# Strassen's seven block products for the first MLP product of a two-layer trunk

## The chip, the cores and the metric

The kernel runs on one core of one Trainium2 chip. Its time is that of one execution on the device, in microseconds (us). The core has five engines that run side by side and meet through semaphores: PE (TensorE, matrix products into the eight banks of PSUM), DVE (VectorE), ACT (ScalarE), POOL (GpSimd) and SP (SyncE, which here only issues DMA transfers between DRAM and the on-chip memory SBUF). DVE and ACT read PSUM and SBUF; POOL works on SBUF alone. A tile is 128 partitions by so many columns, and 512 columns of float32 fill one bank.

## The reference: what is computed

A trunk of two layers works on 1024 positions (tokens) with 1024 features. Layer 0 mixes positions with two recurrent head groups, layer 1 with chunked attention. The rest of a layer is the same for both and is what this change touches:

```
x = x + mix                                   # mix ends in an output projection, 1024 x 1024
hf = rmsnorm(x, norm_ffn_g[i])
x = x + jnp.square(jax.nn.relu(hf @ mlp_w1[i])) @ mlp_w2[i]     # 1024 -> 4096 -> 1024
x = x + rmsnorm(p[i] @ ple_w_proj[i], ple_norm_g[i]) * jax.nn.sigmoid(x @ ple_w_gate[i])
```

The two products of the MLP are each 1024 x 1024 x 4096. The norm's factor per position (rs) can be applied after the first product, since it scales whole positions.

## The kernel before

Everything is kept transposed: features on the partitions, positions on the columns. x is eight tiles of 128 features by 1024 positions, and each is worked on in two halves of 512 positions.

**A product in three.** Float32 operands are split into a high part, rounded to a format that PE multiplies in one pass (float32r), and a low part, the rest. `mm3` (line 276) forms high x high, high x low and low x high: three matmuls of 128x512 for each step of 128 in the sum. A weight tile comes as 512 KB by DMA (`load_w`, line 262) into a buffer `wraw`; ACT casts it to `whi` (line 272), DVE subtracts that to get `wlo` (line 273). `dense_part` (line 288) runs eight (or four) such steps into one PSUM bank and hands it to a function that evacuates it.

**The tail of a layer** is `tail` (line 1152). x is loaded whole into eight SBUF tiles. The output projection runs over its eight output tiles n; the half of the earlier positions is done before, and here only the later half remains, one bank each (tiles 0 and 1 come finished in `self.first`). Its evacuation `ev_out` adds the bank to x, splits x times the norm's weight into the operand `xg` (`split_scaled`, line 309) and adds up the squares of x (`sumsq`, line 320: ACT squares, POOL accumulates).

The MLP goes in eight groups of four tiles of hidden features. `mlp1(g)` makes group g: per tile 2 halves x 8 steps x 3 = 48 matmuls; the evacuation takes the positive part times rs (DVE, line 1222), squares it into the high part (ACT, 1223), squares it again in float32 (POOL, 1224) and subtracts for the low part (DVE, 1225). `mlp2(g)` multiplies the four tiles by the second weights and adds into x (DVE, 1239): 16 banks of 4 x 3 = 12 matmuls. The order is mlp1(0), mlp1(1), mlp2(0), mlp1(2), mlp2(1) and so on; hidden tiles never leave SBUF. Then come the gate's product and the final addition (lines 1265 to 1275).

**What sets the order.** Each engine runs its own queue in order. The order in a queue is made when the program is built: a scheduler goes through time with a model of how long instructions take and, on each engine, issues the earliest instruction of the program that is ready by that model. Buffers are rings: a new tile in a ring waits until all uses of the tile that held the place are done. The first rows of positions' factors (`row_stats`, `to_rows`) are placed by hand after the first and second evacuation of the MLP.

Of the kernel before, what the change touches and what calls it, by code (L numbers as in the profile page):

```python
# [8 lines left out]
F32 = mybir.dt.float32  # L9
F32R = mybir.dt.float32r  # L10
# [7 lines left out]
P = 128  # L18
# [86 lines left out]
class Trunk:  # L105
# [1048 lines left out]
    def tail(self, i, xsrc):  # L1154
        nc, tc, a = self.nc, self.tc, self.a
        V, A, G = nc.vector, nc.scalar, nc.gpsimd
        last = i == 1
        with ExitStack() as es:
# [3 lines left out]
            self.wp = es.enter_context(self.pool(f"wpt{i}", 2))  # L1162
            x = [self.xp.tile([P, 3, T], F32, tag=f"xw{q}", name=f"xw{q}") for q in range(2)]
            x = [x[k // 3][:, k % 3, :] for k in range(6)]
            x += [self.xp.tile([P, T], F32, tag=f"x{k}", name=f"x{k}") for k in (6, 7)]
            self.ht = es.enter_context(self.pool(f"ht{i}"))
            self.sm = es.enter_context(self.pool(f"smt{i}", 2))
            self.slots = {"f": (self.ht, 3)}
            if i == 1:
                self.pre = es.enter_context(self.pool("pre1"))  # L1170
            rs = [None]
            nr = [0]

            def actR():
                q = nr[0] % 8
                nr[0] += 1
                return (self.rx if i == 0 and q < 4 else pB).tile([P, 2, T], F32R, tag=f"r{q}", name="r")

            def actA():
                return self.actA.tile([P, 2, T], F32R, tag="a", name="a")  # L1180

            bt, at = (actR, actA) if i == 0 else (actA, actR)
            hs = [slice(0, HB), slice(HB, T)]
            for k in range(NK):
                nc.sync.dma_start(out=x[k][:, HB:T], in_=xsrc[k][:, HB:T])
            for k in range(NK):
                nc.sync.dma_start(out=x[k][:, 0:HB], in_=self.xh[k])
            accs = [self.accp.tile([P, HB], F32, tag=f"acc{hf}", name="acc") for hf in range(2)]
            col = self.cst.tile([P, NT], F32, tag="col", name="col")
            xg = [at() for _ in range(NK)]  # L1190

            def ev_out(n):
                def f(ps):
                    V.tensor_tensor(x[n][:, hs[1]], x[n][:, hs[1]], ps, op=ALU.add)
# [4 lines left out]
            for n in range(NK):  # L1199
                if n < 2:  # L1200
                    ev_out(n)(self.first[n])
                else:
                    w = self.w_next if (i, n) == (0, 2) else self.load_w(a[f"w_out{i}"][n])
                    yield from self.dense_part(w, self.y, ev_out(n), self.order)

            def rows():
                rs[0] = self.pre.tile([P, T], F32, tag="ph", name="rs")
                self.to_rows(col, rs[0])

            self.late, self.plan = [], {1: lambda: self.row_stats(accs, col), PLAN_ROWS: rows}  # L1210

            xf = [None] * NK

            def mlp1(g):
                hid = []
                for j in range(4):
                    h = bt()
# [535 lines left out]
```

## Time and profile before

| | |
|---|---|
| median of 3 runs | 3310.28 us (3301.96 to 3310.35) |
| profiled execution, its own time | 3307.32 us |
| its span, first to last instruction | 3305.6 us |
| mean granted TensorE clock | 0.972 |
| MLP stages | about 1008 to 1712 (layer 0) and 2510 to 3210 (layer 1) |

How to read the lines of the profile below. PE, PEld (weight loads, which overlap the products), DVE, ACT, POOL and SP are the engines; a q after the name is the engine's sequencer. A group reads: line of the kernel, engine, operation, output<-inputs, shapes, xcount, then busy us and mean ns of one, then idle time just before and what ended it. The answer for one line of the kernel gives the durations as min/median/max in ns and the first and last start. The table of stretches gives for each the busy us of each engine with the number of instructions in brackets, the granted clock (PEclk), the share of DMA engines busy and GB/s. In a timeline the first two columns are start and duration in us. Durations include time in which an engine that has begun an instruction is held up.

### The profile page before, as it was taken

Reading aid. Unit: us, or ns where it says so; the run is one execution under the profiler, and the core shown is the slowest. Engines: PE = TensorE matmul, PEld = TensorE weight load, DVE = VectorE, ACT = ScalarE, POOL = GpSimd, SP = SyncE. Lnnn points to the kernel's source line nnn. Section 1 sums busy time; section 2 is a strip of 40 time slices with the busy share of each in tenths; the row PEclk is TensorE's granted clock in tenths of the full one; section 3 lists DMA queues with packets and bytes.
Section 4 is the critical chain, followed back from the end, with each engine's and each line's share of the span. In section 5 each row is a group of like instructions: output and inputs, shape, how many; then the busy total and the mean of one; then the engine's idle time right before and its main releaser. Section 6 shows DMA issues by size and latency. Waiting matters only on the chain.

```text
span 3305.6 us, 46018 instructions
## 1 busy us (share of the span) xinstructions
PE 3197.8 (97%) x17960; PEld 2639.7 (80%) x17960; DVE 1720.1 (52%) x3550; ACT 1054.5 (32%) x2040; POOL 930.9 (28%) x1262
## 2 busy tenths in 40 slices
PE   7999999999999999999999998889899999999999
PEld 5777777877778888888887988889678888888887
DVE  5566665657554333333357667666854333333344
ACT  4333333334332111111123555555642111111121
POOL 6333533345312101111115335444523111111102
PEclk8999899999889999999999999999999999999999
DMA  3311111222341111111114011010352111111113
GB/s 117 98 60 51 55 55 60 63 69 95 130 138 51 51 45 51 45 51 45 52 64 148 32 44 40 31 34 18 112 204 66 49 46 51 46 51 46 51 46 121
DMA packets 105547, 221.51 MB, mean 67 GB/s; under 512 B 36593, under 2 KB 38769, under 8 KB 105329
## 3 DMA queue, kind: packets, MB, share of 16 engines
q1 hardware_dynamic: 105328, 218.57, 20.0%
q8 instruction: 141, 2.31, 0.3%
q14 instruction: 78, 0.63, 0.1%
HBM read 181.83 MB, written 36.70 MB: 66 GB/s over the span
## 4 chain that ended last, share of the span: by engine, by line
PE 90%; DVE 6%; ACT 2%; issue 1%; DMA 1%; POOL 1%; SPq 0%; DVEq 0%; ACTq 0%; POOLq 0%
PE dps L161 73%; PE ch L161 3%; PE iz L161 2%; PE po L161 2%; PE pm L161 2%; PE tp L161 1%; PE pt L165 1%; PE sn L161 1%; PE py L161 1%; DVE ptile L314 1%; PE pp L161 1%; PE sc L161 1%; PE sf L161 1%; PE dps L165 0%; PE st L161 0%
## 5 line engine op out<-in xcount | busy, mean ns | idle before, releaser
L161 PE MATMUL dps<-a,whi 128*128 128x512 f32 x2304 | 723.3, 394 | 0.0
L161 PE MATMUL dps<-r,whi 128*128 128x512 f32 x2304 | 710.1, 389 | 0.0
L272 ACT CAST whi<-wraw 128x1024 fp32r<-128x1024 f32 x233 | 244.6, 1050 | 1016.7 <-PE dps L161 792.5
L161 PEld LDWEIGHTS dps<-a,whi 128*128 128x128 f32 x2304 | 431.1, 187 | 105.8
L161 PEld LDWEIGHTS dps<-r,whi 128*128 128x128 f32 x2304 | 432.2, 188 | 90.0
L161 PE MATMUL dps<-xg,whi 128*128 128x512 f32 x1360 | 461.7, 416 | 8.4 <-ACT xg L316 7.3
L1224 POOL TENSOR_TENSOR f<-f 128x512 f32<-128x512 f32 x128 | 160.1, 1252 | 1080.2 <-ACT r L1223 541.4
L161 PE MATMUL dps<-a,wlo 128*128 128x512 f32 x1152 | 454.3, 394 | 0.0
L161 PE MATMUL dps<-r,wlo 128*128 128x512 f32 x1152 | 448.2, 389 | 0.0
L273 DVE TENSOR_TENSOR wlo<-wraw,whi 128x1024 fp32r<-128x1024 f32 x233 | 295.3, 1268 | 91.8 <-ACT whi L272 91.6
L161 PEld LDWEIGHTS dps<-xg,whi 128*128 128x128 f32 x1360 | 263.0, 198 | 74.1 <-issue 10.7
L161 PE MATMUL dps<-wq,a 128*128 128x384 f32 x1536 | 304.0, 345 | 5.3 <-DVE vs L1503 3.1
L1239 DVE TENSOR_TENSOR xw<-xw,dps 128x512 f32<-128x512 f32 x192 | 132.0, 688 | 302.5 <-PE dps L161 302.3
L161 PE MATMUL dps<-xg,wlo 128*128 128x512 f32 x680 | 280.9, 413 | 3.1 <-DVE wlo L273 3.1
L161 PEld LDWEIGHTS dps<-wq,a 128*128 128x128 f32 x1536 | 267.0, 191 | 10.4 <-DVE vs L1503 5.3
L1611 POOL TENSOR_SCALAR pb<-pb,l 128x640 f32<-128x640 f32 (+4 forms) x128 | 193.7, 1519 | 248.7 <-DVE l L1610 149.4
L161 PEld LDWEIGHTS dps<-a,wlo 128*128 128x128 f32 x1152 | 215.7, 187 | 53.1
L161 PEld LDWEIGHTS dps<-r,wlo 128*128 128x128 f32 x1152 | 216.2, 188 | 45.0
L1222 DVE SCALAR_TENSOR_TENSOR f<-dps,rs 128x512 f32<-128x512 f32 x128 | 88.3, 691 | 266.3 <-PE dps L161 263.7
L161 PEld LDWEIGHTS dps<-xg,wlo 128*128 128x128 f32 x680 | 133.9, 197 | 35.8 <-issue 4.8
L161 PE MATMUL po<-ptile,vs 128*128 128x256 f32 (+1 forms) x576 | 109.4, 301 | 21.2 <-DVE ptile L314 8.9
L1268 POOL TENSOR_TENSOR pn<-pn,prs 128x512 f32<-128x512 f32 x32 | 48.7, 1524 | 263.2 <-ACT prs L350 177.0
(443 smaller groups left out, 4498.7 us busy)
## 6 DMA issues: line engine op xcount, KB each, us to landing
wraw<-in_w SPq DMA_DIRECT2D x128, 512.0 KB
wraw<-in_w_in SPq DMA_DIRECT2D x56, 512.0 KB
wraw<-in_w_out SPq DMA_DIRECT2D x32, 512.0 KB
wraw<-in_w_qkv SPq DMA_DIRECT2D x24, 512.0 KB
pn<-pnd SPq DMA_DIRECT2D x32, 256.0 KB
wraw<-in_w_gate SPq DMA_DIRECT2D x16, 512.0 KB
yr<-yd SPq DMA_DIRECT2D x30, 256.0 KB
xr<-in_x SPq DMA_DIRECT2D x8, 512.0 KB
```

The costliest lines, as they stand in the source:

```text
L161: return self.nc.tensor.matmul(out, lhsT, rhs, start=start, stop=stop)
L165: return self.nc.tensor.transpose(out, in_, ident)
L272: nc.scalar.copy(hi, raw)
L273: nc.vector.tensor_tensor(lo, raw, hi.bitcast(F32), op=ALU.subtract)
L314: nc.vector.tensor_tensor(dst[:, 1, sl], src, dst[:, 0, sl].bitcast(F32), op=ALU.subtract)
L1222: V.scalar_tensor_tensor(t, ps, 0.0, rs[0][:, sl], op0=ALU.max, op1=ALU.mult)
L1224: G.tensor_tensor(t, t, t, op=ALU.mult)
L1239: V.tensor_tensor(x[n][:, sl], x[n][:, sl], ps, op=ALU.add)
L1268: G.tensor_tensor(pn, pn, prs[:, sl], op=ALU.mult)
L1611: G.tensor_scalar(pb[:, 0:(nf + nn) * P], pb[:, 0:(nf + nn) * P], l[:, 2:3], None, op0=ALU.mult)
```

## The change

The first MLP product is done in pairs of output tiles. A pair's result is cut in 2 x 2 blocks (two tiles of hidden features by two halves of positions), the sum over 1024 features in two halves (even and odd tiles, four steps each). Eight block products would be 8 x 4 x 3 = 96 matmuls; Strassen's method needs seven (84 matmuls), each of a combination of weight blocks with a combination of input blocks, and adds the results up.

- *Inputs.* The seven combinations of the input blocks are built once per layer in `ev_out` and `first_half`, for each couple of x tiles (even and odd), and split into high and low parts: `cmb[1]` to `cmb[7]`. x is no longer held whole: two tiles at a time are loaded (`load_x`), the later half is stored back to DRAM (`xh2`) after the addition, the squares for the norm overwrite the tile. Scaled x goes through one tile `xs` of four quarters.
- *Weights.* `raws(p)` loads the two weight tiles of pair p; `prepare(p, m)` builds combination m in place on POOL (five of the seven need a sum) and splits it on ACT and DVE. It is written one pair ahead.
- *Results.* `product(p, m)` runs 12 matmuls into a bank. ACT copies three of the seven banks out, DVE adds the other four to what is there, POOL does four more sums. Each of the four blocks is then taken to its positive part times rs (DVE), squared (ACT) and stored to DRAM (`hd`).
- *Second product.* It is a stage of its own after all pairs. Squares are loaded back 512 KB at a time and split again (`load_hidden`), four tiles ahead; weights one tile ahead (`load_w2`). x is loaded again from `xh` and `xh2` at the start of that stage.
- *Around it.* The PSUM ring grows from 6 to 8 banks. The pools for weights and evacuation in the tail go; their tiles come from one ring of six tiles (`act`), two more with tag "b", and four tiles called late. Gate weights are loaded after the tile before the last, not ahead of each tile.

The diff, cut to its core:

```diff
+    def act(self, shape, dt, tag="a"):
+        return self.actA.tile(shape, dt, tag=tag, name="act", bufs=6 if tag == "a" else 2)
...
-            self.psd = 2 * self.psd[0:1] + 4 * [es.enter_context(self.pool(f"psdt{i}", 4, space=PSUM))]
+            self.psd = 2 * self.psd[0:1] + 6 * [es.enter_context(self.pool(f"psdt{i}", 6, space=PSUM))]
...
+            def split(c, s):
+                hi, lo = c[:, 0], c[:, 1]
+                if len(s.shape) > 2:
+                    hi, lo = (z.rearrange("p (j c) -> p j c", c=P) for z in (hi, lo))
+                A.copy(hi, s)
+                V.tensor_tensor(lo, s, hi.bitcast(F32), op=ALU.subtract)
...
+            def load_x(n):
+                nc.sync.dma_start(out=xr[n % 2][:, hs[1]], in_=xsrc[n][:, hs[1]])
+                nc.sync.dma_start(out=xr[n % 2][:, hs[0]], in_=self.xh[n])
+
+            def scaled(n, hf):
+                A.activation(xs[:, n % 2, hs[hf]], xr[n % 2][:, hs[hf]], AF.Copy, scale=self.vec("ffng", 8 * i + n))
+            b11, b12, b21, b22 = quarters(xs)
+
+            def first_half(n):
+                scaled(n, 0)
+                if n % 2:
+                    j = n // 2
+                    split(cmb[2][j], b11)
+                    V.tensor_tensor(b21, b21, b11, op=ALU.subtract)
+                    split(cmb[4][j], b21)
 
             def ev_out(n):
                 def f(ps):
-                    V.tensor_tensor(x[n][:, hs[1]], x[n][:, hs[1]], ps, op=ALU.add)
+                    t, j = xr[n % 2], n // 2
+                    V.tensor_tensor(t[:, hs[1]], t[:, hs[1]], ps, op=ALU.add)
+                    nc.sync.dma_start(out=self.xh2[n], in_=t[:, hs[1]])
+                    scaled(n, 1)
+                    if n % 2:
+                        split(cmb[5][j], b22)
+                        V.tensor_tensor(b22, b22, b11, op=ALU.add)
+                        G.tensor_tensor(b12, b12, b11, op=ALU.add)
+                        split(cmb[1][j], b22)
+                        V.tensor_tensor(b11, b12, b22, op=ALU.subtract)
+                        split(cmb[3][j], b11)
+                        split(cmb[6][j], b12)
+                        G.tensor_tensor(b21, b21, b22, op=ALU.add)
+                        split(cmb[7][j], b21)
                     for hf in range(2):
-                        self.split_scaled(xg[n], x[n][:, hs[hf]], self.vec("ffng", 8 * i + n), hs[hf])
-                        self.sumsq(accs[hf], x[n][:, hs[hf]], n == 0)
+                        if n:
+                            A.activation(t[:, hs[hf]], t[:, hs[hf]], AF.Square)
+                            G.tensor_tensor(accs[hf], accs[hf], t[:, hs[hf]], op=ALU.add)
...
+            order = (4, 2, 5, 3, 1, 6, 7)
+            def raws(p):
+                r = place(F32)
+                for e in (1, 0):
+                    nc.sync.dma_start(out=r[:, e], in_=a["w1"][i, 2 * p + e])
...
+                o, u, v, op = {4: (a22, None, None, None), 5: (a12, a12, a11, ALU.add), 2: (a21, a21, a22, ALU.add),
+                               3: (a11, None, None, None), 1: (a22, a22, a11, ALU.add), 6: (a21, a21, a22, ALU.subtract),
+                               7: (a12, a12, a22, ALU.subtract)}[m]
+                if u is not None:
+                    G.tensor_tensor(o, u, v, op=op)
+                split(d[m], o)
...
+            def product(p, m):
+                ps, c = self.bank(), prep[p][1][m]
                 for j in range(4):
+                    o, z = slice(j * P, j * P + P), cmb[m][j]
+                    self.mm3(ps, c[:, 0, o], c[:, 1, o], z[:, 0], z[:, 1], j == 0, j == 3)
+                return ps
...
+            def hidden(t, k, hf):
+                V.scalar_tensor_tensor(t, t, 0.0, rs[:, hs[hf]], op0=ALU.max, op1=ALU.mult)
+                A.activation(t, t, AF.Square)
+                nc.sync.dma_start(out=self.hd[k][:, hs[hf]], in_=t)
...
+            for p in range(16):
+                k = 2 * p
+                if p < 15:
+                    raws(p + 1)
+                for m in order:
+                    ps = product(p, m)
...
+                    if m in (4, 5, 1):
+                        c = scr()
+                        A.copy(c, ps)
+                    if m == 4:
+                        m4 = c
+                    elif m == 2:
+                        c21 = scr()
+                        V.tensor_tensor(c21, m4, ps, op=ALU.add)
+                    elif m == 5:
+                        m5 = c
+                        plus(G, m4, m5, ALU.subtract)
+                    elif m == 3:
+                        plus(V, m5, ps)
+                        f = scr()
+                        G.tensor_tensor(f, m5, c21, op=ALU.subtract)
+                        hidden(c21, k + 1, 0)
+                        hidden(m5, k, 1)
+                    elif m == 1:
+                        plus(G, m4, c)
+                        plus(G, f, m4)
+                    elif m == 6:
+                        plus(V, f, ps)
+                        hidden(f, k + 1, 1)
+                    else:
+                        plus(V, m4, ps)
+                        hidden(m4, k, 0)
+                    if p < 15:
+                        prepare(p + 1, m)
+                    elif m == 5:
+                        load_w2(0)
+                        for j in range(3):
+                            load_hidden(j)
...
+            x = tiles_x(F32)
+            for k in range(NK):
+                nc.sync.dma_start(out=x[k][:, hs[0]], in_=self.xh[k])
+                nc.sync.dma_start(out=x[k][:, hs[1]], in_=self.xh2[k])
...
+            def mlp2(g):
+                hid = H[g % 2]
                 for n2 in range(4):
-                    hi, lo = self.load_w(a["w2"][i, g, n2])
+                    q = 4 * g + n2
+                    hi, lo = w2.pop(q)
+                    if q < 31:
+                        load_w2(q + 1)
+                    if g < 7:
+                        load_hidden(q + 4)
```

More of the change, by code (lines that the diff above doesn't have):

```diff
@@ L1179, in actA @@
[L1179 to L1187, printed above, removed]
+            pB = [pB.tile([P, 2, T], F32R, tag=f"r{q}", name="r") for q in range(8)]
@@ new lines, in tail, with place, lates @@
+            late = es.enter_context(self.pool("late1")) if last else self.rx
+            if last:
+                self.pre = es.enter_context(self.pool("pre1"))
+            self.sm = es.enter_context(self.pool(f"smt{i}", 2))
+            def place(dt, far=False, tag="a"):
+                if far:
+                    return late.tile([P, 2, T], dt, tag=tag, name="late")
+                return self.act([P, 2, T], dt, tag)
+            def lates(dts):
+                return [place(dt, True, f"r{q}") for q, dt in enumerate(dts)]
@@ new lines, in ring, with f, tiles_x @@
+            def ring(views):
+                state = [0]
+                def f():
+                    state[0] += 1
+                    return views[(state[0] - 1) % len(views)]
+                return f
+            halves = lambda t: [t[:, q, :] for q in range(2)]
+            quarters = lambda t: [t[:, q, hs[e]] for q in range(2) for e in range(2)]
+            two = lambda t: t.rearrange("p (q c) -> p q c", q=2)
+            parts = lambda t: [two(v) for v in halves(t)]
+            def tiles_x(dt):
+                xw = [self.xp.tile([P, 3, T], dt, tag=f"xw{q}", name=f"xw{q}") for q in range(2)]
+                return ([xw[k // 3][:, k % 3, :] for k in range(6)] +
+                        [self.xp.tile([P, T], dt, tag=f"x{k}", name=f"x{k}") for k in (6, 7)])
@@ new lines, in tail @@
+            xv = [two(v) for v in tiles_x(F32R)]
+            pq = [c for t in pB for c in parts(t)]
+            cmb = {4: pq[0:4], 2: pq[4:8], 5: xv[0:4], 3: xv[4:8], 1: pq[8:12], 6: pq[12:16],
+                   7: [c for _ in range(2) for c in parts(place(F32R, tag="b"))]}
+            if last:
+                wo, wr, wo2, xr = lates([F32R, F32, F32R, F32])
+            else:
+                wo, wr, wo2, xr = (place(dt) for dt in (F32R, F32, F32R, F32))
+            xs = place(F32)
+            wo, wr, xr = [wo, wo2], halves(wr), halves(xr)
@@ new lines, in weights @@
+            def weights(src, raw, hl):
+                nc.sync.dma_start(out=raw, in_=src)
+                split(hl, raw)
+                return hl[:, 0], hl[:, 1]
+            def load_x(n):
[3 more added lines that the diff above has]
+                A.activation(xs[:, n % 2, hs[hf]], xr[n % 2][:, hs[hf]], AF.Copy, scale=self.vec("ffng", 8 * i + n))
@@ L1258, in tail @@
                 self.xd = [self.dr.tile([P, T], F32, tag=f"xd{k}", name="xd") for k in range(NK)]
-                xg = [at() for _ in range(NK)]
+            scr = ring(quarters(lt[3]))
             def ev_gate(n):
@@ L1417, in load_w @@
             return hi, lo
-        p = [act([P, 2, T], F32R) for _ in range(2)]
+        p = [act([P, 2, T], F32R, "b") for _ in range(2)]
         acc = act([P, 2, HB], F32)
@@ L1459, in load_qkv @@
         for j in range(3):
-            raw = pool.tile([P, T], F32, tag="wraw", name="wraw")
+            raw = place()
             nc.sync.dma_start(out=raw, in_=self.a["w_qkv"][pr, j])
```

134 lines of the change are left out of this document (82 added, 52 removed).

## The prediction, made before the changed kernel was run

> **What bounds the kernel now.** First the page: busy time, the span in slices, the chain of waits.
>
> ```profile
> span 3305.6 us, 46018 instructions
> PE 3197.8 (97%) x17960; PEld 2639.7 (80%) x17960; DVE 1720.1 (52%) x3550; ACT 1054.5 (32%) x2040; POOL 930.9 (28%) x1262
> ...
> PE   7999999999999999999999998889899999999999
> PEclk8999899999889999999999999999999999999999
> ...
> PE 90%; DVE 6%; ACT 2%; issue 1%; DMA 1%; POOL 1%; SPq 0%; DVEq 0%; ACTq 0%; POOLq 0%
> ```
>
> PE carries 90% of the chain that ends last, so work taken from PE counts as long as what feeds it keeps up. Next the busy time by stretch: the two MLPs, the gate stage of layer 0 (1720 to 1780), and the output projection ahead of each MLP (960 to 1000, 2460 to 2480).
>
> ```profile
> core 0: us, PE busy (x) PEld busy (x) DVE busy (x) ACT busy (x) POOL busy (x), PEclk, DMA share, GB/s
> 960.00:980.00 20.00, 16.21 (x62) 12.61 (x62) 17.32 (x31) 11.76 (x18) 4.05 (x3) 0.82 0.23 72
> 980.00:1000.00 20.00, 20.00 (x90) 16.57 (x89) 11.89 (x13) 11.07 (x17) 13.69 (x10) 1.00 0.25 89
> 1008.00:1700.00 692.00, 692.00 (x3022) 564.25 (x3021) 256.37 (x332) 108.31 (x136) 80.06 (x64) 1.00 0.15 48
> 2510.00:3210.00 700.00, 700.00 (x3049) 570.03 (x3048) 260.16 (x333) 111.28 (x141) 80.07 (x64) 1.00 0.14 48
> 1720.00:1740.00 20.00, 20.00 (x90) 16.53 (x90) 13.29 (x13) 8.32 (x13) 6.60 (x4) 1.00 0.38 130
> 1740.00:1760.00 20.00, 20.00 (x90) 16.57 (x89) 16.17 (x13) 8.35 (x14) 12.14 (x8) 1.00 0.42 133
> 1760.00:1780.00 20.00, 20.00 (x90) 16.57 (x89) 14.04 (x13) 9.09 (x14) 10.76 (x8) 1.00 0.51 158
> 2447.00:2460.00 13.00, 13.00 (x58) 10.47 (x57) 2.67 (x4) 2.41 (x4) 1.28 (x1) 1.00 0.91 318
> 2460.00:2480.00 20.00, 17.65 (x75) 13.52 (x74) 16.18 (x18) 13.46 (x20) 7.73 (x4) 1.00 0.39 141
> ```
>
> In the MLPs PE never rests (692 of 692, 700 of 700) at full clock while DVE is busy 37% and POOL 12%: other engines have room. In the projection they have little: DVE 16 to 17 of 20.
>
> The price of one product comes from the evictions of the second MLP product, layer 0:
>
> ```profile
> L1239 DVE TENSOR_TENSOR xw<-xw,dps x96: 686/689/690, 1097.3 to 1700.8; 128x512 f32<-128x512 f32 x96
> L1239 DVE TENSOR_TENSOR x<-x,dps x32: 679/689/690, 1129.9 to 1712.1; 128x512 f32<-128x512 f32 x32
> ```
>
> Between the first (after 12 products of group 0) and the last lie six groups of the first MLP product (6 x 4 x 48 = 1152 matmuls) and 127 evictions of 12 matmuls (1524): 2676 in 614.8 us, **0.230 us each**.
>
> **The change, part by part.**
>
> *Products.* Two output tiles of the first MLP product take 2 x 48 = 96 matmuls now and 7 x 4 x 3 = 84 after, of the same 128x512 form. 16 pairs in each of 2 layers: 384 fewer, 384 x 0.230 = **-88.3 us**. A pair goes from 22.1 to 19.3 us on PE.
>
> *Vector work of a pair.* Durations, from rows:
>
> ```profile
> L1222 DVE SCALAR_TENSOR_TENSOR f<-dps,rs 128x512 f32<-128x512 f32 x128 | 88.3, 691 | 266.3 <-PE dps L161 263.7 <-ACT rs L350 2.6
> L314 DVE TENSOR_TENSOR r<-xw,r x12: 683/691/692, 1672.2 to 1712.7; 128x512 fp32r<-128x512 f32 x12
> L273 DVE TENSOR_TENSOR wlo<-wraw,whi 128x1024 fp32r<-128x1024 f32 x233 | 295.3, 1268 | 91.8 <-ACT whi L272 91.6
> L313 ACT CAST r<-xw x12: 611/621/622, 1671.6 to 1711.2; 128x512 fp32r<-128x512 f32 x12
> L1265 ACT ACTIVATE f<-dps x32: 577/590/601, 1721.7 to 3300.6; 128x512 f32<-128x512 f32 x32
> L1223 ACT ACTIVATE r<-f x64: 623/631/633, 1019.4 to 1625.3; 128x512 fp32r<-128x512 f32 x64
> L328 POOL TENSOR_TENSOR acc<-acc,f x42: 1267/1638/2309, 968.9 to 2502.8; 128x512 f32<-128x512 f32 x42
> L652 POOL TENSOR_TENSOR wraw<-lraw,d_omul x6: 1038/1054/2447, 24.1 to 425.4; 128x512 f32<-128x512 f32 x4, 128x1024 f32<-128x1024 f32 x2
> ```
>
> ACT: 7 casts x 0.62, 3 copies of a bank x 0.59, 4 squares x 0.63 = 8.6 us. DVE: 7 subtractions for the low parts, 4 sums with a bank, 4 relu-and-scale steps, 15 x 0.69 = 10.4 us. POOL: 5 sums of weight tiles and 4 sums of products, 9 x 1.27 (the quickest L328) = 11.4 us. Each fits under 19.3. The weight views step over every other 128 columns, which no such DVE row shows; the strided POOL products of L652 start at 1.04, below the contiguous 1.27, so I add nothing; the other end lies within the 2.5 us a pair taken below.
>
> But DVE and POOL don't work independently. The timeline of the gate stage:
>
> ```profile
> 1738.74 0.32 SPq L1267 DMA_DIRECT2D pn<-pnd  x1
> ...
> 1740.80 1.34 POOL L328 TENSOR_TENSOR acc<-acc,f 128x512 f32<-128x512 f32 x1 [2.63 <-ACT f L327]
> 1741.23 1.45 DVE L1269 SCALAR_TENSOR_TENSOR f<-f,pn 128x512 f32<-128x512 f32 x1 [0.25 <-ACT f L1265]
> 1742.31 1.53 POOL L1268 TENSOR_TENSOR pn<-pn,prs 128x512 f32<-128x512 f32 x1 [0.17 <-DMA pn<-pnd]
> ...
> 1742.72 1.67 DVE L1270 TENSOR_TENSOR xw<-xw,f 128x512 f32<-128x512 f32 x1
> ```
>
> The POOL sum (L328) ends at 1742.14, the DVE step that began inside it at 1742.68, 0.54 later; the next POOL step ends 1.16 after that (1743.84), the next DVE step 0.55 after that (1744.39). So they take turns, 0.55 a DVE turn and 1.16 a POOL turn, when the DVE step reads two SBUF operands. Sums with a bank (L1239: never over 0.690) don't wait. A pair has 7 + 4 = 11 such DVE steps and 9 POOL ones: 11 x 0.55 + 9 x 1.16 = 16.5 us of 19.3, 85%. The gate stage has per tile (48 products, 11.0 us) 6 small and one wide DVE step and 4 POOL steps: 6 x 0.55 + 1.05 + 4 x 1.16 = 9.0, 82%, and there PE stays at 20.00 of 20. So I take PE as the bound of a pair, with 0.3 us for the start of each, **+10 us** in all; bounds 0 (eight banks hold 22 us of products) and 2.5 us a pair, +80 (rival 1).
>
> *Queues.* SP issues two weight loads and four stores a pair, 6 x 0.32 = 1.9 us of 19.3. A store waits on SP for its square, and the next pair's weight load stands behind the last store of a pair, 2.0 us (bank sum, scale, square) into the pair. It lands 3.6 us or a little more later, and its first combination is wanted 19.3 us into the pair: nothing.
>
> The Trainium skill (SBUF — State Buffer, "SBUF: two separate sides") speaks against the change: whoever of the two starts first holds the shared ports for its whole instruction and the other is blocked. The trace agrees on who blocks, but its turns are shorter than whole instructions; by whole ones the sum would move to rival 1.
>
> *The front of a layer.* Now each output-projection tile brings an addition, two scaled splits and two squares. After, a couple of tiles (48 matmuls, 11.0 us) brings, on ACT, 4 scales, 7 casts, 4 squares, 2 wide casts; on DVE 7 subtractions and 3 differences or sums, 2 bank sums, 2 wide subtractions (1.27); on POOL 2 sums and 4 accumulations. DVE and POOL by turns: 10 x 0.55 + 2 x 1.05 + 6 x 1.16 = 14.6 us; by whole durations 10 x 0.69 + 2 x 1.27 + 6 x 1.27 = 17.1. Both are over 11.0. Nor can couples overlap: the scaled inputs sit in one buffer of four quarters, overwritten only after the last split of the couple before, and a tile of x is reloaded only after its square is accumulated. That loop alone (bank sum 0.69, store 3.6 from issue to use as the load of 1738.74 took, square 0.63, accumulation 1.16, load 3.6) is 9.7 us a couple and under the turns. Queued behind are the splits of the next projection weights, and for those PE waits. Four couples, the first ready as now:
>
> ```profile
> 974.74 0.73 PE L161 MATMUL dps<-xg,wh 128*128 128x512 f32 x2 [1.49 <-DVE xw L1194]
> ```
>
> From here six tiles of 24 matmuls end at 974.7 + 144 x 0.230 = 1007.8 now. After, the fourth couple is reached at 974.7 + 3 x 14.6 (or 17.1) = 1018.5 to 1026.0, 10.7 to 18.2 later; I take 15. Then the last couple's sums and pair 0's six weight combinations (13 DVE turns, 9 POOL turns: 7.2 + 10.4 = 17.6 us) run against six products (16.6 us), and the row statistics wait for the last accumulation: 5 us. Together **20 us a layer, +40**. Bounds: 5 (if the order of issue finds gaps, as now, where PE loses 3.8 us of 960 to 980), and 38 (18.2 plus 20 for a first pair that also carries pair 1's weights and its own sums: 24 DVE and 18 POOL turns, 34 us against 19.3).
>
> The projection now shows a clock of 0.82 where PE idled 3.8 us, and 1.00 where it idled 2.35. The Trainium skill (TensorE: Matmul & The Clock Gate, Part 1) has an idle window of about 3.4 us halve the clock until one busy window has passed; by it, every stall of that length costs about 1.7 us more, and three in each front would make the sum some 10 us larger, 3288.
>
> *The second product as its own stage.* Same matmuls. Per weight tile (48 matmuls, 11.0 us) it splits two wide tiles and adds four banks: DVE 2 x 1.27 + 4 x 0.69 = 5.3, ACT 2.1, POOL none: hidden. The squares leave and return, 16.8 MB each way per layer: 2 MB a pair, 2.1 / 19.3 = 109 GB/s, and 1.05 MB per 11.0 us = 95 GB/s, under the 318 GB/s that 2447 to 2460 carried. At the seam 4.2 MB of x are issued on SP ahead of the second weight tile, once the combinations in their space are read, 3 products (8.3 us) before the seam: 13.2 us at 318 GB/s puts them 5 us past it, with 11 us of work at hand. I take 3 us a layer, **+6**; bounds 0 and 10 (half the rate: 26 - 8 = 18 us past the seam, and 2.3 for the split, less the 11 at hand). Dropped squares and splits on ACT, POOL and DVE of now are hidden under PE: no gain. Gate stage and attention do the same work: nothing.
>
> *Sum.* The profiled execution took 3307.3 us (span 3305.6); 3307.3 - 88.3 + 40 + 10 + 6 = 3275. The median of the runs is 3310.3, 3 above it, so **3278 us**.
>
> **Rivals.** 1. *DVE and POOL become the bound in the pairs* (slower). If turns last whole instructions (11 x 0.69 + 9 x 1.27 = 19.0) and bank sums find no POOL step to lie under, a pair takes 19.0 + 4 x 0.69 = 21.8 us and nothing is saved: 3278 + 32 x 2.5 - 10 = 3348. For it: L328 steps stretch from 1.27 to 2.31. Against: the gate stage. It decides above 19.3 + (88.3 - 46) / 32 = 20.6 us a pair. 2. *The front is hidden*, 5 us a layer: 3278 - 30 = 3248; for it, DVE steps here are already issued out of program order into gaps; against, there are no gaps at 14.6 of 11.0. 3. *The front costs its upper bound*, 38 a layer: 3278 + 36 = 3314, no change. That the saving isn't there at all is excluded: matmuls are counted.
>
> **How the numbers follow.** Forecast 0.55 (its own range 3255 to 3298), rival 1 0.17, rival 2 0.17, rival 3 0.11. A change under 0.3% (10 us) can't be told from none here; faster is forecast and rival 2, 0.72, same is rival 3, 0.11, slower is rival 1, 0.17. Range 3238 to 3328: all of rivals 2 and 3, and the mild end of rival 1.
>
> **What would show it.** 17576 matmuls in place of 17960. In the first product PE at 20 of 20 and a pair every 19.3 us says PE is the bound; DVE near full with PE waiting on DVE or POOL says rival 1. The fourth couple's additions 10 to 18 us later than now say the front is right. A PE wait on a weight split or an `hd` load at the seam over 5 us a layer says the seam is wrong. The prediction fails above all if pairs take over 20.6 us.

## The result, and the profile after

The changed kernel takes **3329.56 us** (median, 3327.89 to 3330.39), the kernel before, timed beside it, 3310.32 (3301.96 to 3310.91): a ratio of 1.0063 with a 95% interval of 1.0046 to 1.0081. It is slower. The forecast was 3278 and faster, its range 3238 to 3328.

The page of the changed kernel, the lines that answer to those shown of before: span and busy time, PE and its clock in slices, the chain that ended last by engine.

```profile
span 3328.7 us, 46709 instructions
PE 3150.4 (95%) x17576; PEld 2578.3 (77%) x17576; DVE 2100.8 (63%) x3822; ACT 1264.2 (38%) x2416; POOL 1254.1 (38%) x1438
...
PE   7999999999988999999999998889897999999999
PEclk8999999999988999999999999999997999999999
...
PE 66%; DVE 15%; POOL 7%; DMA 5%; issue 3%; ACT 3%; SPq 0%; ACTq 0%; DVEq 0%; POOLq 0%
```

The 384 matmuls are gone (17576 for 17960), yet PE's busy time fell by 47 us only, and its share of the chain went from 90% to 66%. What took the place is DVE, POOL and DMA, 27% together for 8% before. The busy time by stretch says where: the front of layer 0 (960 to 1060), the pairs (1100 to 1360), the seam (1360 to 1380), the second product (1400 to 1600) and the front of layer 1 (2480 to 2560).

```profile
core 0: us, PE busy (x) PEld busy (x) DVE busy (x) ACT busy (x) POOL busy (x), PEclk, DMA share, GB/s
960.00:1060.00 100.00, 81.45 (x307) 62.57 (x308) 88.18 (x90) 54.10 (x93) 64.74 (x40) 0.83 0.36 121
1100.00:1360.00 260.00, 245.10 (x1041) 193.41 (x1040) 189.28 (x182) 95.56 (x168) 166.36 (x107) 1.00 0.28 99
1360.00:1380.00 20.00, 17.04 (x53) 11.80 (x53) 16.40 (x17) 9.68 (x12) 7.86 (x4) 0.70 1.03 390
1400.00:1600.00 200.00, 200.00 (x859) 162.01 (x858) 91.19 (x108) 38.38 (x37) 0.00 (x0) 1.00 0.28 95
2480.00:2560.00 80.00, 62.01 (x226) 47.12 (x225) 74.69 (x77) 42.57 (x73) 54.02 (x33) 0.79 0.32 105
```

The second product runs as forecast, PE 200 of 200. The front loses PE time and clock. The pairs are the surprise: PE rests, but neither DVE (189 of 260) nor POOL (166 of 260) is near full. Their pace is read from the one addition that each pair makes at line 1367 (16 pairs, 15 intervals); under it stand the additions of the output projection at the front (1251), the last step of the recurrence (1148) and the additions of the second product (1419).

```profile
L1367 DVE TENSOR_TENSOR late<-late,dps x16: 672/674/686, 1034.5 to 1359.4; 128x512 f32<-128x512 f32 x16
L1251 DVE TENSOR_TENSOR act<-act,dps x8: 673/676/689, 962.6 to 1017.1; 128x512 f32<-128x512 f32 x8
L1148 DVE SCALAR_TENSOR_TENSOR o<-o,d_hgdn x8: 742/749/752, 294.0 to 959.0; 128x512 f32<-128x512 f32 x8
L1419 DVE TENSOR_TENSOR x<-x,dps x32: 680/689/689, 1404.1 to 1726.1; 128x512 f32<-128x512 f32 x32
```

(1359.4 - 1034.5) / 15 = **21.66 us a pair**, where 84 matmuls need 19.3. (The first two intervals belong to the start; the 13 from the third addition, at 1079.2, to the last are 21.6 each.) The chain of waits between 1228 and 1296 shows what a pair waits for, in order of time (start, us, what):

```profile
by line: POOL act L1293 33.3%; DMA act<-in_w 19.1%; DVE late L1326 15.1%; DVE act L1224 13.2%; issue 9.3%; POOL late L1323 5.5%; DVE late L1323 3.0%; ACT act L1223 2.7%; SPq L1277 1.0%; ACT late L1327 0.1%; POOLq L1293 0.1%
...
1243.90 0.70 DVE act L1224
...
1245.01 4.78 DMA act<-in_w
...
1251.28 1.76 POOL act L1293
...
1253.10 3.33 POOL act L1293 x2
1256.44 1.25 POOL late L1323
1257.71 0.69 DVE late L1323
1258.40 2.30 DVE act L1224 x2
1260.70 3.42 DVE late L1326 x2
...
1265.31 0.70 DVE act L1224
1266.03 3.63 DMA act<-in_w
```

PE itself waits often and briefly in the pairs, for casts (1223) and low parts (1224) that have only just been made, and for a bank (1323). From 1180 to 1360 (us in total, times, longest):

```profile
PE dps L161 <- ACT act L1223: 4.4, 7, 0.7
PE dps L161 <- DVE act L1224: 4.1, 8, 0.5
PE dps L161 <- DVE late L1323: 3.0, 8, 0.8
```

No matmul is in the chain. It is a ring: the last low part of a pair's weights (1265.31, line 1224) lets the next pair's weights be loaded (1266.03), POOL waits for them and makes its sums (1293), DVE splits them by turns with POOL and between its bank sums and scale steps, and the last split comes 21.41 us after the one before. So the theory of the runs below, called L: the loop through the tile of raw weights sets the pace. Its rivals: T, the turns of DVE and POOL set it (the mild end of the prediction's rival 1); S, the SP queue, where loads stand behind stores that wait for squares; and, for the loss outside the pairs, the seam and the DRAM traffic.

Two sections of the span measure each part later: from the last step of the recurrence to the last addition of the second product (layer 0), and from the last attention output (line 1846 of the changed kernel) to the same (layer 1). The fewer matmuls alone would take 44.2 us from each.

| us | layer 0 | layer 1 |
|---|---|---|
| before | 966.2 to 1712.1: 745.9 | 2443.5 to 3210.4: 766.9 |
| after | 959.0 to 1726.1: 767.1 | 2459.4 to 3234.8: 775.4 |

### The profile page after: what moved, and what is told of

Its sections match the earlier page's. It is cut to its first block, busy times and chain, and to the rows that moved or that the text cites. A ratio compares the mean times of both kernels' runs of the same rounds, so it can differ in the third digit from the quotient of the medians.

```text
span 3328.7 us, 46709 instructions
## 1 busy us (share of the span) xinstructions
PE 3150.4 (95%) x17576; PEld 2578.3 (77%) x17576; DVE 2100.8 (63%) x3822; ACT 1264.2 (38%) x2416; POOL 1254.1 (38%) x1438
## 4 chain that ended last, share of the span: by engine, by line
PE 66%; DVE 15%; POOL 7%; DMA 5%; issue 3%; ACT 3%; SPq 0%; ACTq 0%; DVEq 0%; POOLq 0%
PE dps L161 50%; POOL act L1293 5%; DMA act<-in_w 4%; DVE act L1224 4%; DVE late L1326 3%; PE ch L161 3%; PE iz L161 2%; PE po L161 2%; PE pm L161 2%; PE tp L161 1%; PE pt L165 1%; POOL late L1323 1%; PE sn L161 1%; DVE r L1224 1%; PE py L161 1%
## 5 line engine op out<-in xcount | busy, mean ns | idle before, releaser
L161 PE MATMUL dps<-r,act 128*128 128x512 f32 x3528 | 851.1, 399 | 43.6 <-ACT r L1223 15.3
L161 PEld LDWEIGHTS dps<-r,act 128*128 128x128 f32 x3528 | 669.1, 191 | 214.1 <-ACT r L1223 18.0
L1224 DVE TENSOR_TENSOR act<-act 128x512 fp32r<-128x512 f32 (+1 forms) x309 | 380.6, 1250 | 116.7 <-ACT act L1223 114.9
L161 PE MATMUL dps<-late,act 128*128 128x512 f32 x1536 | 356.3, 394 | 0.0
L161 PEld LDWEIGHTS dps<-late,act 128*128 128x128 f32 x1536 | 289.4, 188 | 65.6
L1223 ACT CAST act<-act 128x512 fp32r<-128x512 f32 (+1 forms) x309 | 221.2, 728 | 297.8 <-PE dps L161 167.8
L1293 POOL TENSOR_TENSOR act<-act 128x512 f32<-128x512 f32 x160 | 254.1, 1604 | 188.7 <-DMA act<-in_w 180.1
L161 PE MATMUL dps<-wq,act 128*128 128x384 f32 x1536 | 301.7, 343 | 3.5 <-DVE vs L1696 2.5
L161 PEld LDWEIGHTS dps<-wq,act 128*128 128x128 f32 x1536 | 264.9, 190 | 8.2 <-DVE vs L1696 4.2
L276 ACT CAST whi<-wraw 128x1024 fp32r<-128x1024 f32 x78 | 81.7, 1047 | 122.8 <-PE dps L161 78.2
```

The costliest lines, as they stand in the source:

```text
L161: return self.nc.tensor.matmul(out, lhsT, rhs, start=start, stop=stop)
L276: nc.scalar.copy(hi, raw)
L1223: A.copy(hi, s)
L1224: V.tensor_tensor(lo, s, hi.bitcast(F32), op=ALU.subtract)
L1293: G.tensor_tensor(o, u, v, op=op)
```

## The experiments

Each time is a median, with its ratio to the kernel before, timed on the same chip, and the 95% interval of the ratio. "Run 1" and so on are these numbers; run 5 is its first kernel.

**1. Two places for the raw weights.** The ring of six is cut to four, and two places alternate for the raw tiles.

```diff
-        return self.actA.tile(shape, dt, tag=tag, name="act", bufs=6 if tag == "a" else 2)
+        return self.actA.tile(shape, dt, tag=tag, name="act", bufs={"a": 4, "b": 2}.get(tag, 1))
...
-                r = place(F32)
+                r = place(F32, tag=f"w{p % 2}")
```

> The changed kernel with two places of their own for the raw weight tiles of a pair (w0, w1, taken from the ring of six), so that the next pair's load need not wait for the last split out of the same place. Vector work is unchanged. Theory A (a loop through the one raw tile: load 4.8 us, then 16.5 us of sums and splits, one after the other, make the 21.4 us pace of the pairs): the pace falls to what PE needs, 19.3 to 19.7 us, and the time to 3265 to 3285 us. Rival B (the turns of DVE and POOL alone make 21.4 us a pair): pace 21.2 to 21.6 and time 3322 to 3336 us, as before this edit.

Measured: 3361.72 us, 1.016 [1.0132, 1.0189] of before. Neither theory's number. Successive pairs still come 21.5 us apart (1084.57, 1106.07, 1127.67), and between 1150 and 1300 POOL waits for the loads (us in total, times, longest):

```profile
POOL act L1293 <- DMA act<-in_w: 59.8, 9, 9.0
```

(The answer for the changed kernel between 1200 and 1340, nearly as long a stretch, has 44.7 us in 10 times for the same wait.) The order of issue in the built program tells why. The scheduler places POOL's first two sums of the newest raw tile ahead of the rest of the pair's POOL work, and that rest includes the last three sums of the tile before, which lies in the other place. POOL works in order, so everything behind stands in line for a load of the same pair. The other place therefore comes free only at the end, and the next load leaves right behind the last low part out of it:

```profile
1195.76 1.29 POOL L1293 TENSOR_TENSOR act<-act 128x512 f32<-128x512 f32 x1 [8.52 <-DMA act<-in_w]
1197.36 2.55 POOL L1293 TENSOR_TENSOR act<-act 128x512 f32<-128x512 f32 x2 [0.31 <-DMA act<-in_w]
...
1212.26 0.69 DVE L1224 TENSOR_TENSOR act<-act 128x512 fp32r<-128x512 f32 x1
...
1213.01 0.83 SPq L1277 DMA_DIRECT2D act<-in_w  x2
```

A second place does not help as long as its work waits for the load into the first. The 32 us that the run lies above the changed kernel are mostly at the front of layer 1, where the last additions of the output projection (line 1251) come at 2565.8 for 2529.4; a ring of four is short there, but which tile is late was not followed up.

**2. The new stage alone.** The kernel before with its plain products, its squares stored to DRAM and the second product a stage of its own. x stays in SBUF in this run, so its way through DRAM is not part of it.

```diff
-                        A.activation(h[:, 0, sl], t, AF.Square)
-                        G.tensor_tensor(t, t, t, op=ALU.mult)
-                        V.tensor_tensor(h[:, 1, sl], t, h[:, 0, sl].bitcast(F32), op=ALU.subtract)
+                        A.activation(t, t, AF.Square)
+                        nc.sync.dma_start(out=hd[k][:, sl], in_=t)
...
+            for g in range(8):
+                yield from mlp1(g)
+            for k in range(4):
+                load_hidden(k)
+            for g in range(8):
+                yield from mlp2(g, H[4 * g:4 * g + 4])
```

> The kernel before with one part of the change alone: all of the first product (plain, 96 matmuls a pair of tiles) first, its squares stored to DRAM, then the second product as a stage of its own, which loads and splits them again; POOL's second square and the old low part of the squares are gone. Theory A (the way through DRAM is hidden, the seam between the stages costs a stall of 5 to 11 us a layer with the half clock after it): 3315 to 3335 us, and PE busy all along within each stage. Rival B (the loads and splits of the second stage also hold PE up): PE waits on splits in the second stage and the time is over 3340 us. Rival C (seam and DRAM are free): 3304 to 3314 us.

Measured: 3304.31 us, 0.9994 [0.9981, 1.0007]. No difference, and PE has no rest across the seam at 1360:

```profile
1000.00:1360.00 360.00, 360.00 (x1557) 290.50 (x1556) 91.73 (x113) 78.90 (x104) 3.31 (x3) 1.00 0.30 99
1360.00:1380.00 20.00, 20.00 (x90) 16.47 (x89) 9.18 (x11) 5.54 (x7) 0.00 (x0) 1.00 0.49 158
```

The squares' way through DRAM is free by itself, so the loss has to be looked for in the pairs and the front.

**3. No sums of squares on POOL.** The changed kernel without POOL's additions for the norm.

```diff
                             A.activation(t[:, hs[hf]], t[:, hs[hf]], AF.Square)
-                            G.tensor_tensor(accs[hf], accs[hf], t[:, hs[hf]], op=ALU.add)
```

> The changed kernel with POOL's accumulation of the squares of x left out in the output projection for all tiles but the first (the factors of the norm are then not those of the reference). Theory A (the front is bound by the turns of DVE and POOL): 14 turns of 1.16 us a layer go, the fourth couple's addition comes 10 to 14 us earlier in each layer, and the time is 3300 to 3312 us. Rival B (the front is bound by the one buffer of scaled inputs and the reload of x, chains that DVE's own steps make): at most 6 us a layer, 3317 to 3330 us.

Measured: 3294.78 us, 0.9958 [0.9943, 0.9973], 35 us under the changed kernel, more than either theory gave. At the front of layer 0 PE has more work and more clock (the changed kernel has 13.91 at 0.93 and 13.20 at 0.56 in these two stretches):

```profile
1000.00:1020.00 20.00, 16.88 (x81) 13.45 (x79) 18.52 (x25) 17.92 (x34) 10.57 (x7) 1.00 0.38 132
1020.00:1040.00 20.00, 17.07 (x64) 13.18 (x65) 18.75 (x28) 8.15 (x15) 12.90 (x8) 0.83 0.20 66
```

The fourth couple's last addition comes 48.0 us behind the recurrence's last step for 58.1 in the changed kernel, 10 earlier as theory A has it, and the first pair's addition 75.5 - 67.1 = 8.4 us earlier in layer 0 and 6.0 in layer 1. The first two intervals of the pairs, which still belong to the start, shrink from 44.7 and 45.3 us to 37.3 and 33.3. Together this is 34 of the 36 us by which the two sections get shorter. The 13 intervals behind are 21.6 and 21.5 us each, as in the changed kernel: the pace of the pairs has not moved. So POOL's additions were a part of the front and of the pairs' start, dearer than theory A put them, and the loop is still there.

**4. The stores from ACT's queue.** One line: in `hidden`, the store of the square is issued by ACT and not by SP.

```diff
-                nc.sync.dma_start(out=self.hd[k][:, hs[hf]], in_=t)
+                nc.scalar.dma_start(out=self.hd[k][:, hs[hf]], in_=t)
```

> The changed kernel with the stores of the squares issued from ACT's queue, behind the square itself, in place of SP's; one raw weight place as before. Theory L (a pair is held by its loop: last split out of the raw tile, load, POOL sums, splits): the load of the next weights no longer stands behind stores that wait for squares, but it still waits for the last split, so the pace stays 21.2 to 21.6 us and the time 3320 to 3332. Theory S (the queue of SP is what holds the load): the pace falls under 20.6 and the time under 3305. Theory T (turns of DVE and POOL set the pace): 21.4 us, 3325 to 3335.

Measured: 3344.57 us, 1.0123 [1.0107, 1.0138], a pair every (1372.1 - 1037.3) / 15 = 22.3 us: slower still, past both numbers, and against S. What it shows is the wait itself. In the changed kernel SP's waits between 1100 and 1340 were these (us in total, times, longest):

```profile
SPq L1328 <- ACT late L1327: 201.3, 44, 13.8
SPq L1277 <- DVE act L1224: 8.5, 11, 0.8
```

With the stores gone from SP, the time moves to the load (line 1277), which, once the load before has landed, waits for the last low part (1224) 16.8 us in every pair:

```profile
SPq L1277 <- DVE act L1224: 167.8, 10, 17.3
```

The stores had only hidden it.

**5. POOL's sums held in order, with two raw places.** The kernel of run 1, and each POOL sum of the pairs is bound to follow the one before it in the program.

```diff
+            def queued(f, bind=True):
+                if queue[0] is None or not bind:
+                    r = f()
+                else:
+                    with tc.issue_after(queue[0]):
+                        r = f()
+                queue[0] = r.ins
...
-                    G.tensor_tensor(o, u, v, op=op)
+                    queued(lambda: G.tensor_tensor(o, u, v, op=op), p > 0)
```

> The changed kernel with two raw weight places (and four in place of six in the common ring), and POOL's sums held in the order of the program, so that the first sum of the newest weight tile stands behind all POOL work of the pair in which it was loaded, not ahead of it. Theory L (loop through the raw tile): the weights are there a whole pair ahead, the pace falls to 19.3 to 19.9 us, and from the 3362 of the kernel with two raw places alone about 32 x 1.8 = 57 us go, 3295 to 3320, with what the ring of four costs at the front left in. Theory T (turns of DVE and POOL): the pace stays 21.2 to 21.6 whatever is loaded when, and the time 3345 to 3365.

Measured: **3289.17 us**, 0.9948 [0.9929, 0.9967], 72.6 under run 1. Over 260 us of pairs PE has no rest, with the same vector work:

```profile
L1381 DVE TENSOR_TENSOR late<-late,dps x16: 672/676/680, 1036.6 to 1319.7; 128x512 f32<-128x512 f32 x16
...
1060.00:1320.00 260.00, 260.00 (x1135) 212.62 (x1134) 204.84 (x207) 112.31 (x192) 187.02 (x123) 1.00 0.30 110
```

(1319.7 - 1036.6) / 15 = 18.9 us. The first pairs come late and the next catch up; the last eleven intervals are 19.3 each, so the pairs are bound by PE. DVE and POOL are busier than in the changed kernel (205 and 187 of 260, for 189 and 166) and hold nothing up: T is out. With the stores on ACT's queue as well:

> The same as the run with POOL's sums in order and two raw places, and also the stores of the squares issued from ACT's queue, so that nothing on SP stands ahead of a weight load but loads. Theory L: as that run or up to 10 us less (the load then leaves as soon as its place is free), 3288 to 3320 with a pace of 19.3 to 19.7. Theory T: pace 21.2 to 21.6, 3345 to 3365.

Measured: 3293.73 us, 0.997 [0.9956, 0.9983]; the intervals overlap, and the queue of the stores makes no difference that can be told.

**6. The order alone, and the order with one fixed place.** Run 5 without run 1's places, in the ring of six, called the order alone from here on:

> The changed kernel with only the order of POOL's sums held, and one raw weight place and the ring of six as they were: the half of the remedy that the run with two places alone did not have. Theory L (loop through the raw tile): the load still leaves only after the last split out of the tile, so the pace stays 21.0 us or more and the time 3318 to 3345. If the order alone does it (the place is no part of the loop), the pace falls under 19.9 and the time under 3290.

Measured: **3255.00 us**, 0.9845 [0.9826, 0.9864], 75 under the changed kernel: the second case of the expectation, (1325.3 - 1035.9) / 15 = 19.29 us a pair.

```profile
L1380 DVE TENSOR_TENSOR late<-late,dps x16: 673/675/690, 1035.9 to 1325.3; 128x512 f32<-128x512 f32 x16
...
1060.00:1320.00 260.00, 260.00 (x1135) 212.62 (x1134) 187.66 (x205) 111.39 (x191) 182.90 (x125) 1.00 0.32 110
1320.00:1400.00 80.00, 80.00 (x351) 65.60 (x350) 51.76 (x57) 29.34 (x33) 8.91 (x6) 1.00 0.62 218
```

Was the place then no part of it? The addresses in the built programs say that this run changed both. In the changed kernel every raw weight tile of the pairs gets the same address (in layer 1 from the second on); with the sums held in order the planner moves it round the ring (pairs 2 to 8 at six different addresses), and the wait of the load on the low parts is gone from SP's list. So a last run holds the order and pins the place: one fixed buffer for raw weights, a ring of five for the rest.

```diff
+        return self.actA.tile(shape, dt, tag=tag, name="act", bufs={"a": 5, "b": 2}.get(tag, 1))
...
-                r = place(F32)
+                r = place(F32, tag="w0")
```

> The changed kernel with POOL's sums held in order, and one fixed place for every raw weight tile (a ring of five for the rest): in the run with the order alone the planner gave the raw tile a place that moved round the ring, so order and place changed together. Theory L (the loop through the raw tile: a load waits for the last split of the tile before, then sums and splits of all seven combinations, the last of them 16 us later): the pace is 20.9 us or more though the order holds, and the time 3300 to 3345. Theory O (the order of POOL's sums alone sets the pace): 19.3 to 19.6 us, and 3250 to 3290.

Measured: 3337.93 us, 1.0088 [1.0067, 1.0109], (1362.2 - 1035.0) / 15 = 21.81 us a pair, as L says. PE rests again with less of everything done in the same time, and the chain shows the ring, from a last low part to the load and on to the next one:

```profile
1100.00:1360.00 260.00, 241.55 (x1006) 185.90 (x1005) 184.11 (x181) 96.90 (x168) 166.45 (x108) 0.99 0.28 98
...
1210.05 0.69 DVE act L1224
1210.76 3.96 DMA act<-in_w
...
1231.22 0.69 DVE act L1224
1231.92 5.88 DMA act<-in_w
```

The stretch left out between these lines holds 5.33 us of matmuls on weights just split, so this ring runs in part through PE.

Counted alike, over the 13 intervals from the third addition of layer 0 on: the changed kernel 21.6 us a pair; two places without the order 21.6; the order without a second place 21.8; both, in run 5 and with the order alone, 19.0. Each half alone leaves the loop closed, once through the buffer and once through POOL's queue. (The ring for the rest had five places here and six in the order alone; with four, in run 5, the pairs still ran at 19.0.)

**7. The front.** Squares summed by PE in place of POOL, on the kernel of run 5: 32 more matmuls with a matrix of ones collect them in two banks.

```diff
-                            G.tensor_tensor(accs[hf], accs[hf], t[:, hs[hf]], op=ALU.add)
...
+                        self.mm(sqb[hf], self.onesr, accr[hf], n == 0, n == NK - 1)
```

> The kernel with two raw places and POOL's sums in order, and the sum of squares of x at the front of a layer taken off POOL: the squares go to TensorE, which adds them up over the eight tiles in two banks with a matrix of ones (32 matmuls of 128x512 in all, 7.4 us), so 14 POOL additions a layer go. Theory F (the front is held by turns of DVE and POOL, and the halved clock after PE's rests multiplies what is lost): 10 x 0.55 + 2 x 1.05 + 2 x 1.16 = 9.9 us of turns a couple stand under the 11.0 us of its matmuls, PE at 17 of 20 and over with clock 0.8 to 1.0 at the fronts, and about 35 us less, as leaving the additions out of the changed kernel gave: 3250 to 3262. Theory D (DVE alone, or the latency of one couple's chain, holds the front): DVE stays at 19 to 20 of 20 and PE under 15 of 20 there, 3280 to 3297.

Measured: 3263.16 us, 0.9872 [0.9854, 0.9890]. 26 us under run 5, one above F's range and far from D's. The front of layer 1, which the ring of four had made worst, in run 5 and then here (the 60 us around the last couples):

```profile
2480.00:2540.00 60.00, 29.37 (x64) 17.34 (x65) 57.13 (x63) 35.33 (x63) 41.60 (x26) 0.52 0.29 97
```

```profile
2470.00:2530.00 60.00, 38.89 (x139) 27.86 (x140) 46.38 (x67) 37.32 (x67) 23.23 (x15) 0.69 0.27 98
```

In the first PE is busy half of the time at half of its clock, so 29.4 x 0.52 = 15 us of work in 60. DVE is full at 57 of 60. Relieving POOL relieves DVE, which does the same work in the second with 46. On the order alone, with the ring of six:

> The changed kernel with POOL's sums held in order and the squares of x summed by TensorE, in the ring of six. Theory L + F (the loop of the weight tile set the pace, turns of DVE and POOL with the halved clock the front): the two gains add up, 3255 - 26 (what the sums on TensorE gave with two raw places) to 3255 - 35, 3220 to 3232, with a pace of 19.3 and PE at 16 to 20 of 20 at the fronts. If both remedies worked on the same loss: 3245 to 3258.

Measured: **3249.99 us**, 0.9833 [0.9809, 0.9857], the lowest median of all, but 5 us under the order alone and not 26: the second case. Its interval overlaps that of the order alone, so a gain is not shown. In layer 0 the way from the recurrence's end to the first pair falls from 73.2 to 69.1 us, in layer 1, from the last attention output, from 88.4 to 85.7. With the ring of four the way in layer 1 had been 135.4 in run 5 and 112.7 with the squares on PE. So most of the 26 was damage of the ring of four at the front of layer 1, which the ring of six does not have. Last, a second buffer for the scaled inputs, so that couples can overlap (layer 0 takes it from the tiles called late, layer 1 from the ring):

```diff
-            xs = place(F32)
+            xsb = [place(F32), place(F32) if last else place(F32, True, "r0")]
```

> The kernel with POOL's sums in order and the squares summed by TensorE, and a second buffer for the scaled inputs of the front, so that a couple of tiles can begin before the last split of the couple before has read its quarters. Theory T (what is left at the front is the turns of DVE and POOL, or DVE alone): the couples still come 13 us apart and the time stays within 6 us of 3250, 3244 to 3256. Theory B (couples that can't overlap, the one buffer of four quarters): the couples come 11 to 12 us apart, PE over 18 of 20 at the fronts, 3228 to 3243.

> The kernel with POOL's sums in order and the squares still summed by POOL, with the second buffer for the scaled inputs. Theory T (turns of DVE and POOL hold the front): as without the buffer, 3249 to 3261, the couples 14 us apart or more. Theory B (couples that can't overlap): 3230 to 3248, and then the sums of squares cost little once the buffer is there.

Measured: 3259.12 us (0.9846 [0.9828, 0.9864]) and 3266.81 (0.9870 [0.9855, 0.9884]): nothing gained. The medians lie 9 and 12 us higher, a little past T's numbers, but the intervals overlap those without the buffer. So a second buffer taken in this way does not free the front, and B is not borne out. That DVE and POOL's turns alone hold it is not shown either: the rest of the front's cost stays open between the turns, the clock and the order of issue.

## Why the prediction was wrong, point by point

**The step that failed is "*Queues*".** It asked what stands ahead of the next pair's weight load on SP, found the last store, 2.0 us, and priced the load at nothing, since its first combination is wanted 19.3 us into the pair. It left out what the load itself waits for: its buffer. The place was held by the raw weights of the pair before, until their last combination was made and split. In the changed kernel PE begins a pair at 1248.98, on weights that have only just been split; the load for the next pair leaves at 1266.03, not 2 but 17 us later, and lands at 1269.66. PE begins the next pair on it at 1270.44: nothing is left of the lead of one pair. Five sums and seven splits follow the landing before the place is free again (in run 4 this takes 16.8 us a pair), and the next load takes 3.6 to 4.8. The loop is 21.4 us. And POOL's queue closes the same loop a second time (run 1). Its price: from the order alone to the changed kernel 767.1 - 727.9 = 39 us in layer 0 and 775.4 - 744.1 = 31 in layer 1, 70 of the 75 us between the two spans.

| us | layer 0 | layer 1 |
|---|---|---|
| order alone (6) | 962.7 to 1690.6: 727.9 | 2415.8 to 3159.9: 744.1 |
| and squares on PE (7) | 967.3 to 1687.8: 720.5 | 2415.0 to 3154.9: 739.9 |
| order held, one place (6) | 964.4 to 1733.0: 768.6 | 2463.8 to 3243.9: 780.1 |

**Products: right.** 384 matmuls are gone, and with the order alone PE does 1135 matmuls in 260 us, 0.229 each, which makes 19.2 us for a pair's 84. In the changed kernel PE's busy time fell by 47 us only; multiplied by the mean granted clock (0.972 before, 0.961 after) it fell by 81, so by this estimate most of the rest are matmuls that ran at a lower clock.

**Vector work of a pair: right in its verdict.** It took PE as the bound with the turns at 85%, and with the loop open PE is at 260 of 260 with the same steps on DVE and POOL. The start of a pair costs nothing there that shows, not 0.3. In the changed kernel the durations are stretched by turns, as in these rows between 1060 and 1360, but stretched steps are not a bound:

```profile
L1293 POOL TENSOR_TENSOR act<-act x67: 1274/1635/1847, 1058.5 to 1340.4; 128x512 f32<-128x512 f32 x67
L1326 DVE SCALAR_TENSOR_TENSOR late<-late,rs x58: 680/1232/1791, 1060.2 to 1353.6; 128x512 f32<-128x512 f32 x58
```

**Rival 1 had the right pace for the wrong reason.** It gave 21.8 us a pair and 3348; the pace was 21.66. That the vector work sets the pace is refuted by runs 5 and 6. Behind it stood the rule of the Trainium skill (SBUF — State Buffer, "SBUF: two separate sides") that the one who starts holds the ports for its whole instruction. The pace of 19.29 excludes the 21.8 that it gave with the bank sums on top; whole turns alone, 19.0, would just fit, so the pace does not decide on the rule. The longest hold-ups in the two rows, 1.791 - 0.680 = 1.11 us for DVE and 1.847 - 1.274 = 0.57 for POOL, are under a whole step of the other (1.27 and 0.68), as the turns in the gate stage were. Over the whole execution, though, line 1293 reaches 2.05, which is 0.77 over its shortest and more than a step of 0.68, so the length of a turn stays open.

**The front: right in size.** Forecast were 20 us a layer, with 5 for the pairs' starts and 3 for the seam 28. With the loop open, the order alone is 727.9 - (745.9 - 44.2) = 26 us over what the matmuls alone give in layer 0, and 744.1 - 722.7 = 21 in layer 1. The fourth couple's additions came at 1017.1, under the forecast 1018.5 to 1026.0; counted from the recurrence's last step, which came 7 us earlier, they are 58.1 us behind it, near the upper end of the forecast's 52.3 to 59.8. One reading under it was off: the prediction has DVE at 16 to 17 of 20 in the projection, but its row from 980 to 1000 shows 11.9. What the front is made of was not foreseen either: the halved clock is a part of it. With the order alone the last 20 us of layer 0's front read

```profile
1020.00:1040.00 20.00, 12.74 (x35) 9.02 (x36) 19.16 (x20) 9.86 (x18) 12.93 (x9) 0.50 0.28 94
```

so 12.7 busy us at 0.50 are 6.4 us of work: 6.4 are lost to the clock beside 7.3 to the rests. The Trainium skill (TensorE: Matmul & The Clock Gate, Part 1) has the clock halve after an idle window of about 3.4 us; a side sentence priced that at 1.7 us for each of three stalls a front. The trace agrees that it halves, but where rests come one after another it stays low for whole stretches, and the cost is 6 us in this one.

**The seam: free**, not 3 us. Run 2 and the order alone, which does load x again, pass it with PE at its full time (20 of 20, and 80 of 80 from 1320). What the changed kernel loses there (17.04 at clock 0.70) is gone with the loop.

**The sum.** 3278 forecast, 3255 with the loop open, 3330 with it closed. Of the 52 us between the spans of the kernel before and the order alone, 41 lie in the two sections; the other 11 lie outside them and were not followed up, so the 3255 does not confirm every term. Rivals 2 and 3 were about the front; the case that happened, a buffer that admits its next load too late, was not among the rivals, though the price of a slow pair (over 20.6 us decides) was.

## What to carry to other kernels

For each load that is "a step ahead", ask first what must have happened to the buffer it lands in, then what stands ahead of it in the queue; and follow the loop once round: release, load, sums, splits, release. A loop longer than the step sets the pace although no engine in it is full, and the sign is a chain that goes from load to sums to splits to load with little or nothing of the engine that ought to bound, while that engine rests a little in every step (PE at 94% here, DVE at 73%, POOL at 64%). Two things can close the same loop, a buffer and the order of an in-order queue, and taking one away alone shows nothing.

## What the runs showed of the hardware and was not expected

Where PE rests again and again, the granted clock stays at 0.50 to 0.56 for 20 to 60 us (0.52 from 2480 to 2540 in run 5). A front that keeps PE at about 17 of 20 had 0.83 to 1.00 (run 3). Of two that kept it at 13 to 14 of 20, one had 0.50 (the order alone, 1020 to 1040) and the other 0.93 (the changed kernel, 1000 to 1020). So the busy share of such a stretch does not tell its clock.

A busy DVE or POOL is partly a waiting one: steps of 0.68 us were shown at up to 1.79 and steps of 1.27 at up to 1.85 where the two met. DVE at 19 to 20 of 20 at the fronts therefore did not mean that its work filled the time; with POOL's sums of squares gone (run 7, in the ring of six) DVE was busy 75 of the 100 us from 960 to 1060 with 105 instructions, with the order alone 85 with 96.
